# A decoder layer on one core: the recurrence's small products in three groups a chunk in place of six, nine early products, and halved first splits

## Chip, cores, metric

One core of a Trainium2 chip runs the whole program. The metric is device time in microseconds (us) of one execution; the time before is the median of three runs. TensorE is called PE in the profile, VectorE DVE, ScalarE ACT, GpSimd POOL, and SyncE, whose queue issues most transfers, SP.

## The reference

One layer over 1024 tokens of width 1024, in float32. A projection `p = x @ W_in` of 4864 columns is cut into nine parts: q, f, i, g of a gated recurrence (4 heads of 128), q, k, v of a sliding-window attention, and two branch gates of 1024 columns each. Then

```
logf = log(lb + (1 - lb) * sigmoid(f));  k = 1 - exp(logf)
per chunk:  b = cumsum(logf)
  scores[t,s] = sum_k q[t,k] * exp(b[t,k] - b[s,k]) * k[s,k]      (s <= t)
  o = (q * exp(b)) @ state + scores @ v
  state = exp(b_last) * state + (k * exp(b_last - b)).T @ v
o = rms_norm(o) * norm_w * silu(g)
merged = sigmoid(ga) * (o @ W_a) + sigmoid(gb) * (attention @ W_b)
x = layer_norm(alpha * x + merged @ W_out)
x = layer_norm(alpha * x + mixture of 32 experts, two per token, of width 512)
```

## The kernel before

**Numbers.** A float32 operand is split into a high half (ScalarE casts it) and a low half (VectorE subtracts the high one): `split`, line 97. A product of two split operands is three matrix instructions into one PSUM bank (`mm3`, lines 101 to 105: high by high, high by low, low by high; the profile calls them L103, L104, L105). They are called big products here: 128x128 weights, 512 columns. Small products of the recurrence are plain fp32; the trace has two records for each of those products, and one for each transpose.

**Stages.** A Tile planner orders the work: in the first two stages TensorE's instructions run in the order of the program, and the planner orders the other engines' queues by program order and its own estimate of when things are ready. Each engine then executes its queue in that order. After these two stages come mixing (branch products, first norm, router) and the experts, where all five engines keep the order of the program.

*Start* (`att_proj`, line 243). SP issues the loads of x (eight of 512 KB), of the first weights and of constants. `first` (line 265) takes four x chunks in turn: split the chunk (`split_x`), at chunks 0 and 2 split also 512 KB of weights (`wsplit_half`), then issue the products of two of eight k slices for two column tiles: 12 big products a chunk, 48 in all. ScalarE copies each finished column tile out of PSUM (`keep`, L259). Then the second half of x is split and multiplied (`query`).

*Stage 1* computes attention, with the projection for the recurrence as filler. *Stage 2* (from about 303 us to 532 us of the span) computes the recurrence, with the projection of the branch gates as filler: eight columns of weights, 768 big products. `weave` (line 231) deals the filler over the entries of a list: before entry i it issues filler until `start + i * (total - start) / len(main)` units are out. A unit is an estimate of time in the program; the three instructions of one k slice count 0.64. In stage 2 `total` is 164 and `start` is 8.

**The recurrence** (`hgrn`, line 520) goes over eight chunks n of 128 tokens. The lower triangle of the scores is made by levels: at level h (1, 2, 4, ..., 64) each block of 2h tokens gives the products of its later half with its earlier half. `prep_level` makes the operands on ScalarE and VectorE (two exponentials; subtract, two multiplies, add: L571 to L579), each level continuing on the running sums `hl` that the level before it left. `level` and `diag` issue small products of 32 or 64 columns, and `keep` (L538) copies them by a mask into the score tile `hst`, four instructions a level on VectorE. `decay` transposes the decayed keys; `output(n)` multiplies scores by values and queries by the state, then squares on ScalarE, sums on VectorE, takes a power on GpSimd (L701) and scales on VectorE into `ho` (L668); `state(n)` makes the next state; `out(n)` transposes `ho` (L414) and stores it.

These calls stand in a list of groups, sorted by a place: for a chunk n, in this order, levels 1, 2 with the diagonal; output and state of chunk n-1; levels 4, 8; out of chunk n-1; levels 16, 32; level 64 and decay. That is 48 groups. The preparation of a group is issued two groups ahead of it. `load(n + 1)`, five loads of 256 KB, is issued with the preparation of levels 16, 32 of chunk n. Three entries of `mixing_start` (loads and splits for the next stage) are inserted 8, 6 and 4 places from the end, so the list has 51 entries.

**Buffers.** The tiles of the recurrence share one ring of 24 (`s2`); operands of the levels, weights and x share 36 of 4 KB a partition (`q4`); five PSUM banks (`pb`) serve the groups, three (`mm`) the big products.

Of the kernel before, what the change touches and what calls it, by code (L numbers as in the profile page):

```python
# [5 lines left out]
F32 = mybir.dt.float32  # L6
# [55 lines left out]
class Builder:  # L62
# [34 lines left out]
    def split(self, hi, lo, src, eng=None):  # L97
        self.nc.scalar.copy(hi, src)  # L98
        (eng or self.nc.vector).tensor_sub(lo, src, hi.bitcast(F32))  # L99

    def mm3(self, out, lh, ll, rh, rl, start, stop):
        mm = self.nc.tensor.matmul
        mm(out, lh, rh, start=start, stop=False)  # L103
        mm(out, lh, rl, start=False, stop=False)  # L104
        mm(out, ll, rh, start=False, stop=stop)  # L105
# [61 lines left out]
    def split_x(self, half, raws):  # L167

        self.xh.append([])
        self.xl.append([])  # L170
        for raw in raws:
            h, l = self.q4([128, 2, 512], F32R, "xh"), self.q4([128, 2, 512], F32R, "xl")
            self.split(h, l, raw)
            self.xh[half].append(h)
            self.xl[half].append(l)
            yield
# [13 lines left out]
    def wsplit(self, raws):  # L190
        return [self.wsplit_half(raw) for raw in raws]

    def wsplit_half(self, raw):
        h = self.q4([128, 4, 256], F32R, "wh")
        l = self.q4([128, 4, 256], F32R, "wl")
        self.split(h, l, raw)
        return h, l

    def proj_T(self, w, ct, half):
# [43 lines left out]
    def att_proj(self):  # L243
        nc = self.nc
        self.xh, self.xl = [], []
        x0 = [self.load_x(0, 0)]
        raw = [self.wload_half(2048, 0)]
        x0.append(self.load_x(0, 1))
        raw.append(self.wload_half(2048, 1))
        x0 += [self.load_x(0, j) for j in (2, 3)]  # L250
        x1 = [self.load_x(1, j) for j in range(4)]
        raw2 = self.wload(2304)
        self.setup_more()
        raw3 = self.wload(2560)
        self.aq = [self.q4([128, 4, 256], name=f"aq{i}") for i in range(4)]

        def keep(ps, ch, ct, half):
            for b in range(2):
                nc.scalar.activation(self.aq[2 * half + b][:, 2 * ch + ct], ps[:, 256 * b:256 * b + 256], AF.Copy, scale=0.125)  # L259

        def query(w, ch, half):
            for ct in range(2):
                keep(self.run(self.proj_T(w, ct, half)), ch, ct, half)

        def first():

            w, xs = [], self.split_x(0, x0)
            gens = [self.proj_T(w, ct, 0) for ct in range(2)]
            for j in range(4):
                next(xs)  # L270
                if j % 2 == 0:
                    w.append(self.wsplit_half(raw[j // 2]))
                for _ in range(2):
                    for gen in gens:
                        next(gen)
            for ct, gen in enumerate(gens):
                keep(self.run(gen), 0, ct, 0)
            return w

        w = first()  # L280
        for _ in self.split_x(1, x1):
            pass
        query(w, 0, 1)
        w = self.wsplit(raw2)
        for half in range(2):
            query(w, 1, half)
        w = self.wsplit(raw3)
        self.ak = self.q4([128, T], name="ak")
        self.av = self.tile([128, 8, 2, 2, 64], F32R, "av", 1)
        self.ksh = self.tile([128, 2, 2, 128], F32R, "ksh", 1)  # L290
        self.ksl = self.tile([128, 2, 2, 128], F32R, "ksl", 1)
        vts = []
        for half in range(2):
            s = slice(half * 512, half * 512 + 512)
            ps = self.run(self.proj_T(w, 0, half))
            nc.scalar.copy(self.ak[:, s], ps)
            ps = self.run(self.proj_T(w, 1, half))
            vt = self.st2()
            nc.scalar.copy(vt, ps)
            vts.append(vt)  # L300
        for half, vt in enumerate(vts):
            tp = self.bank("pa", (128, 4, 128))
            for i in range(4):
                nc.tensor.transpose(tp[:, i], vt[:, i * 128:i * 128 + 128], self.c("ident"))
            av = self.av[:, 4 * half:4 * half + 4]
            self.split(av[:, :, :, 0], av[:, :, :, 1], tp.rearrange("p i (g d) -> p i g d", g=2))
# [213 lines left out]
    def hgrn(self):  # L520
# [3 lines left out]
        nc = self.nc  # L524
# [15 lines left out]
        def load(n):  # L540
            t0 = slice(n * 128, n * 128 + 128)
            for nm, src in (("hl", self.hl[:, :, t0]), ("hk", self.hk[:, :, t0]), ("hq", self.hq[:, :, t0]),
                            ("hv", self.hv[t0].rearrange("p (h k) -> p h k", h=4)),
                            ("hg", self.hg[t0].rearrange("p (h k) -> p h k", h=4))):
                V[nm, n] = self.tile([128, 4, 128], F32, nm, 2)
                nc.sync.dma_start(V[nm, n], src)
# [6 lines left out]
        def prep_diag(n):  # L553
            V["st", n] = self.tile([128, 4, 128], F32, "hst", 2)
            nc.gpsimd.memset(V["st", n], 0.0)
# [48 lines left out]
        def prep_levels(n, hs):  # L604
            t = self.q4([128, 2, 512], F32, "hE")
            es = [t[:, j].rearrange("p (h x) -> p h x", h=4) for j in range(2)]
            for h, e in zip(hs, es):
                prep_level(n, h, e)

        def levels(n, hs):  # L610

            pp = self.bank("pb", (128, 4, 128))
            posts = [diag(n, pp)] if hs[0] == 1 else []
            posts += [level(n, h, pp, j) for j, h in enumerate(hs)]
            for post in posts:
                post()
# [57 lines left out]
        none = lambda: None  # L674
        groups = []
        for n in range(8):
            at = 4 * n
            groups += [(at, lambda n=n: (prep_diag(n), prep_levels(n, (1, 2))), lambda n=n: levels(n, (1, 2))),
                       (at + 1, lambda n=n: prep_levels(n, (4, 8)), lambda n=n: levels(n, (4, 8))),
                       (at + 2, lambda n=n: (n < 7 and load(n + 1), prep_levels(n, (16, 32))), lambda n=n: levels(n, (16, 32))),  # L680
                       (at + 3, lambda n=n: (prep_levels(n, (64,)), prep_decay(n)), lambda n=n: (levels(n, (64,)), decay(n))),
                       (at + 4.5, none, lambda n=n: (output(n), state(n))),
                       (at + 5.5, none, lambda n=n: out(n))]
        groups.sort(key=lambda t: t[0])
        load(0)
        ahead = 2
        for _, pre, _ in groups[:ahead]:
            pre()

        def group(i):  # L690
            if i + ahead < len(groups):
                groups[i + ahead][1]()
            groups[i][2]()

        return [lambda i=i: group(i) for i in range(len(groups))]

# [748 lines left out]
    def build(self):  # L1445
        pool = self.tc.tile_pool
        with pool(name="base", bufs=1) as self.base, pool(name="dr", bufs=1, space=DRAM) as self.dr:
            self.setup()
            self.n2 = 13
            self.banks = {"mm": 3, "sc": 1, "pa": 3}  # L1450
            with pool(name="sb1", bufs=1, reuse_waits="tile") as self.sb, \
                    pool(name="ps1", bufs=1, space=PSUM, reuse_waits="tile") as self.ps, self.pe_order():
                self.att_proj()
                self.hg_consts()
                stream = self.stream()
                self.weave(self.attention(), stream, 164)
            self.n2 = 24
            self.banks = {"mm": 3, "pb": 5}
            with pool(name="sb2", bufs=1, reuse_waits="tile") as self.sb, \
                    pool(name="ps2", bufs=1, space=PSUM, reuse_waits="tile") as self.ps, self.pe_order():  # L1460
                groups = self.hgrn()
                for n, fn in zip((8, 6, 4), self.mixing_start()):
                    groups.insert(len(groups) - n, fn)
                self.weave(groups, stream, 164, 8)
            self.n2 = 4
            with pool(name="sb3", bufs=1, reuse_waits="tile") as self.sb:
                self.banks = {"mm": 4, "pa": 1, "tb": 1, "pb": 2}
                with pool(name="ps3", bufs=1, space=PSUM, reuse_waits="tile") as self.ps:
                    with self.all_order():
                        self.mixing()  # L1470
                        self.slots()
                    self.overflow()
                self.banks = {"mm": 4, "pb": 4}
                with pool(name="ps4", bufs=1, space=PSUM, reuse_waits="tile") as self.ps, self.all_order():
                    self.moe()
# [44 lines left out]
```

## Time and profile before

| | |
|---|---|
| median of three runs | 1399.96 us (1399.85 to 1399.97) |
| profiled execution | 1399.95 us |
| its span (first to last instruction) | 1398.2 us |
| mean granted TensorE clock | 0.984 |
| PE busy, share of the span | 1335.6 us, 96% |
| weight loads (PEld) | 1100.5 us, 79% |
| VectorE | 1080.5 us, 77% |
| ScalarE | 789.4 us, 56% |
| GpSimd | 241.8 us, 17% |
| transferred | 327.84 MB, mean 234 GB/s |

Times count from the first instruction. Busy times of an engine are the union of its instructions; matrix instructions are pipelined, so their durations overlap: what a stretch of products costs is read from the starts. The page cuts the span into 40 slices of 35 us. Its busy line for TensorE shows 7 tenths in the first slice, 9 or more from there on, and 8, 4, 4 in the last three; VectorE's shows 8 and 9 in slices 4 to 6 (stage 1) and 10 to 14 (most of stage 2), mostly 5 and 6 from there to the experts, and 9 through the experts.

### The profile page before, as it was taken

What the parts mean: (1) busy time and instruction counts of PE and PEld (TensorE: products, weight loads), DVE (VectorE), ACT (ScalarE), POOL (GpSimd) and SP (SyncE); (2) the same over time, 40 slices, a digit from 0 to 9 for tenths busy, and PEclk for the clock granted to TensorE, in tenths of its full rate; (3) what the DMA queues carried; (4) which work ended last, traced back from release to release, by engine and by line L of the source; (5) the groups of instructions that cost most, each with busy time, mean ns of one, the idle gap of its engine ahead of it and who ended that gap; (6) DMA issues with size and microseconds to landing.
All of it is one profiled execution on the core that took longest, in us unless ns stands there. A gap on an engine that the chain in (4) does not pass through costs nothing. (4 is left out here: it accounts for less than half of the span.)

```text
span 1398.2 us, 22818 instructions
## 1 busy us (share of the span) xinstructions
PE 1335.6 (96%) x8314; PEld 1100.5 (79%) x8314; DVE 1080.5 (77%) x1798; ACT 789.4 (56%) x1282; POOL 241.8 (17%) x160
## 2 busy tenths in 40 slices
PE   7999999999999999999998999999999999999844
PEld 5888899987788887788787888888888888888621
DVE  4268985779989956668656989999999999999645
ACT  4367644335545532312112888888888888888542
POOL 0001312120000002300001122222222222222123
PEclk9999999999999999999999999999999999999967
DMA  6124232153444436763557999999999999999962
GB/s 246 56 89 145 100 112 76 39 169 114 137 128 146 148 103 194 254 211 121 196 195 287 356 368 369 366 356 354 353 357 358 352 358 357 367 360 365 369 251 97
DMA packets 142564, 327.84 MB, mean 234 GB/s; under 512 B 18614, under 2 KB 59702, under 8 KB 142448
## 3 DMA queue, kind: packets, MB, share of 16 engines
q1 hardware_dynamic: 132800, 308.78, 60.9%
q0 software_dynamic: 9648, 17.57, 4.9%
q8 instruction: 66, 1.08, 0.3%
q14 instruction: 50, 0.41, 0.1%
HBM read 291.43 MB, written 52.43 MB: 246 GB/s over the span
## 5 line engine op out<-in xcount | busy, mean ns | idle before, releaser
L99 DVE TENSOR_TENSOR el<-er,eh 128x1024 fp32r<-128x1024 f32 x368 | 436.8, 1223 | 53.4 <-ACT eh L98 37.8
L98 ACT CAST eh<-er 128x1024 fp32r<-128x1024 f32 x368 | 369.7, 1054 | 99.5 <-PE mm L104 82.7
L103 PE MATMUL mm<-xh,wh 128*128 128x512 f32 x480 | 194.9, 406 | 7.8 <-ACT wh L98 6.8
L103 PE MATMUL mm<-eh,xh 128*128 128x512 f32 x496 | 196.4, 396 | 0.0
L104 PE MATMUL mm<-el,xh 128*128 128x512 f32 x496 | 196.2, 395 | 0.0
L105 PE MATMUL mm<-eh,xl 128*128 128x512 f32 x496 | 196.1, 395 | 0.0
L104 PE MATMUL mm<-xl,wh 128*128 128x512 f32 x480 | 189.0, 394 | 0.8 <-DVE xl L99 0.8
L105 PE MATMUL mm<-xh,wl 128*128 128x512 f32 x480 | 189.1, 394 | 0.0
L103 PEld LDWEIGHTS mm<-xh,wh 128*128 128x128 f32 x480 | 91.4, 190 | 25.7 <-ACT wh L98 6.8
L105 PEld LDWEIGHTS mm<-eh,xl 128*128 128x128 f32 x496 | 93.2, 188 | 22.5
L104 PEld LDWEIGHTS mm<-el,xh 128*128 128x128 f32 x496 | 93.2, 188 | 22.3
L103 PEld LDWEIGHTS mm<-eh,xh 128*128 128x128 f32 x496 | 93.2, 188 | 22.3
L105 PEld LDWEIGHTS mm<-xh,wl 128*128 128x128 f32 x480 | 91.2, 190 | 20.6 <-DVE wl L99 0.8
L1086 POOL DMA_INDIRECT xg<-x1d,gi x32 | 58.1, 1816 | 279.3 <-PE pb L1149 255.4
L104 PEld LDWEIGHTS mm<-xl,wh 128*128 128x128 f32 x480 | 91.4, 190 | 17.7 <-DVE xl L99 1.1
L103 PE MATMUL mm<-eh,hth 128*128 128x512 f32 x240 | 100.2, 418 | 0.0
L1090 POOL DMA_INDIRECT zd<-y,gi x29 | 69.8, 2407 | 156.5 <-ACT y L1240 156.5
L105 PE MATMUL mm<-eh,htl 128*128 128x512 f32 x240 | 94.8, 395 | 0.0
L104 PE MATMUL mm<-el,hth 128*128 128x512 f32 x240 | 94.8, 395 | 0.0
L103 PE MATMUL mm<-wh,xh 128*128 128x256 f32 x256 | 73.1, 286 | 0.0
L105 PE MATMUL mm<-wh,xl 128*128 128x256 f32 x256 | 72.4, 283 | 0.0
L104 PE MATMUL mm<-wl,xh 128*128 128x256 f32 x256 | 72.4, 283 | 0.0
(257 smaller groups left out, 2522.7 us busy)
## 6 DMA issues: line engine op xcount, KB each, us to landing
er<-w_g SPq DMA_DIRECT2D x128, 512.0 KB
er<-w_u SPq DMA_DIRECT2D x128, 512.0 KB
er<-w_d SPq DMA_DIRECT2D x128, 512.0 KB
wr<-w_in SPq DMA_DIRECT2D x38, 512.0 KB
gated<-st SPq DMA_DIRECT2D x32, 256.0 KB
st<-gated SPq DMA_DIRECT2D x32, 256.0 KB
xr<-xt SPq DMA_DIRECT2D x8, 512.0 KB
wab<-w_a SPq DMA_DIRECT2D x16, 256.0 KB
```

What stands on the lines that cost most here:

```text
L98: self.nc.scalar.copy(hi, src)
L99: (eng or self.nc.vector).tensor_sub(lo, src, hi.bitcast(F32))
L103: mm(out, lh, rh, start=start, stop=False)
L104: mm(out, lh, rl, start=False, stop=False)
L105: mm(out, ll, rh, start=False, stop=stop)
L1086: self.nc.gpsimd.indirect_dma_start(to, None, rows, bass.IndirectOffsetOnAxis(ap=self.column(self.gi, e), axis=0), bounds_check=T - 1, oob ...
L1090: self.nc.gpsimd.indirect_dma_start(self.zd, bass.IndirectOffsetOnAxis(ap=idx, axis=0), y, None, bounds_check=T - 1, oob_is_err=False, com ...
```

## The change

The edit has three parts. A new `early` fills a 128x128 tile with ones and issues nine fp32 products of it with itself into a bank that nobody reads, ahead of `first`. A new `split_parts` splits a tile in two halves along its second dimension, each with its own cast and subtraction; it is used for the first x chunk and the first weight half. The groups of the recurrence are put together in threes a chunk: levels 1, 2 with output and state of chunk n-1; levels 4, 8 with out of chunk n-1; levels 16, 32, 64 with decay. Two more groups end the list, so it has 26, and with the three inserted entries (5, 4 and 2 places from the end) 29. Preparation is still issued two groups ahead; `load(n + 1)` now goes with the preparation of the third group.

```diff
--- before.py
+++ after.py
@@ -98,6 +98,12 @@
         self.nc.scalar.copy(hi, src)
         (eng or self.nc.vector).tensor_sub(lo, src, hi.bitcast(F32))
 
+    def split_parts(self, hi, lo, src):
+
+        n = src.shape[1] // 2
+        for s in (slice(0, n), slice(n, 2 * n)):
+            self.split(hi[:, s], lo[:, s], src[:, s])
+
     def mm3(self, out, lh, ll, rh, rl, start, stop):
         mm = self.nc.tensor.matmul
         mm(out, lh, rh, start=start, stop=False)
@@ -170,7 +176,7 @@
         self.xl.append([])
         for raw in raws:
             h, l = self.q4([128, 2, 512], F32R, "xh"), self.q4([128, 2, 512], F32R, "xl")
-            self.split(h, l, raw)
+            (self.split if half or self.xh[0] else self.split_parts)(h, l, raw)
             self.xh[half].append(h)
             self.xl[half].append(l)
             yield
@@ -190,10 +196,10 @@
     def wsplit(self, raws):
         return [self.wsplit_half(raw) for raw in raws]
 
-    def wsplit_half(self, raw):
+    def wsplit_half(self, raw, first=False):
         h = self.q4([128, 4, 256], F32R, "wh")
         l = self.q4([128, 4, 256], F32R, "wl")
-        self.split(h, l, raw)
+        (self.split_parts if first else self.split)(h, l, raw)
         return h, l
 
     def proj_T(self, w, ct, half):
@@ -262,6 +268,14 @@
             for ct in range(2):
                 keep(self.run(self.proj_T(w, ct, half)), ch, ct, half)
 
+        def early():
+
+            t = self.tile([128, 128], F32, "early", 1)
+            nc.vector.memset(t, 1.0)
+            ps = self.bank("mm")
+            for _ in range(9):
+                nc.tensor.matmul(ps[:, 0:128], t, t, start=True, stop=True)
+
         def first():
 
             w, xs = [], self.split_x(0, x0)
@@ -269,7 +283,7 @@
             for j in range(4):
                 next(xs)
                 if j % 2 == 0:
-                    w.append(self.wsplit_half(raw[j // 2]))
+                    w.append(self.wsplit_half(raw[j // 2], j == 0))
                 for _ in range(2):
                     for gen in gens:
                         next(gen)
@@ -277,6 +291,7 @@
                 keep(self.run(gen), 0, ct, 0)
             return w
 
+        early()
         w = first()
         for _ in self.split_x(1, x1):
             pass
@@ -674,23 +689,21 @@
         none = lambda: None
         groups = []
         for n in range(8):
-            at = 4 * n
-            groups += [(at, lambda n=n: (prep_diag(n), prep_levels(n, (1, 2))), lambda n=n: levels(n, (1, 2))),
-                       (at + 1, lambda n=n: prep_levels(n, (4, 8)), lambda n=n: levels(n, (4, 8))),
-                       (at + 2, lambda n=n: (n < 7 and load(n + 1), prep_levels(n, (16, 32))), lambda n=n: levels(n, (16, 32))),
-                       (at + 3, lambda n=n: (prep_levels(n, (64,)), prep_decay(n)), lambda n=n: (levels(n, (64,)), decay(n))),
-                       (at + 4.5, none, lambda n=n: (output(n), state(n))),
-                       (at + 5.5, none, lambda n=n: out(n))]
-        groups.sort(key=lambda t: t[0])
+            groups += [(lambda n=n: (prep_diag(n), prep_levels(n, (1, 2))),
+                        lambda n=n: (levels(n, (1, 2)), n and (output(n - 1), state(n - 1)))),
+                       (lambda n=n: prep_levels(n, (4, 8)), lambda n=n: (levels(n, (4, 8)), n and out(n - 1))),
+                       (lambda n=n: (n < 7 and load(n + 1), prep_levels(n, (16, 32)), prep_levels(n, (64,)), prep_decay(n)),
+                        lambda n=n: (levels(n, (16, 32)), levels(n, (64,)), decay(n)))]
+        groups += [(none, lambda: (output(7), state(7))), (none, lambda: out(7))]
         load(0)
         ahead = 2
-        for _, pre, _ in groups[:ahead]:
+        for pre, _ in groups[:ahead]:
             pre()
 
         def group(i):
             if i + ahead < len(groups):
-                groups[i + ahead][1]()
-            groups[i][2]()
+                groups[i + ahead][0]()
+            groups[i][1]()
 
         return [lambda i=i: group(i) for i in range(len(groups))]
 
@@ -1459,7 +1472,7 @@
             with pool(name="sb2", bufs=1, reuse_waits="tile") as self.sb, \
                     pool(name="ps2", bufs=1, space=PSUM, reuse_waits="tile") as self.ps, self.pe_order():
                 groups = self.hgrn()
-                for n, fn in zip((8, 6, 4), self.mixing_start()):
+                for n, fn in zip((5, 4, 2), self.mixing_start()):
                     groups.insert(len(groups) - n, fn)
                 self.weave(groups, stream, 164, 8)
             self.n2 = 4
```

## Rows read from the trace of the kernel before

**Rows 1.** Busy us by stretch (instructions): PE, PEld, DVE, ACT, POOL; clock, DMA share, GB/s
```profile
23.20:26.40 3.20, 3.01 (x7) 2.46 (x8) 2.93 (x4) 2.26 (x3) 0.00 (x0) 0.53 0.33 88
...
379.68:460.20 80.52, 80.52 (x1010) 66.05 (x1003) 73.87 (x211) 38.71 (x91) 6.06 (x12) 1.00 0.43 137
...
490.00:530.00 40.00, 40.00 (x397) 33.62 (x384) 22.89 (x66) 12.72 (x26) 2.20 (x3) 1.00 0.28 86
800.00:1300.00 500.00, 500.00 (x2322) 407.37 (x2321) 451.06 (x440) 407.84 (x496) 119.36 (x55) 1.00 0.99 360
```

**Rows 2.** Timeline of the start: start us, duration us, engine, line, operation
```profile
4.43 1.05 ACT L98 CAST xh<-xr 128x1024 fp32r<-128x1024 f32 x1 [2.40 <-DMA xr<-xt]
...
5.67 1.05 ACT L98 CAST wh<-wr 128x1024 fp32r<-128x1024 f32 x1 [0.19 <-DMA wr<-w_in]
...
6.77 0.80 PE L103 MATMUL mm<-xh,wh 128*128 128x512 f32 x1 [6.77 <-ACT wh L98]
...
8.02 0.80 PE L105 MATMUL mm<-xh,wl 128*128 128x512 f32 x1
...
9.05 0.63 PE L104 MATMUL mm<-xl,wh 128*128 128x512 f32 x1
...
9.47 0.63 PE L105 MATMUL mm<-xh,wl 128*128 128x512 f32 x1
...
12.80 1.22 DVE L99 TENSOR_TENSOR wl<-wr,wh 128x1024 fp32r<-128x1024 f32 x1
...
13.23 0.39 PE L105 MATMUL mm<-xh,wl 128*128 128x512 f32 x1
```

**Rows 3.** The same timeline, end of the first block and what follows
```profile
20.74 0.39 PE L105 MATMUL mm<-xh,wl 128*128 128x512 f32 x1
...
22.13 0.50 PE L103 MATMUL mm<-xh,wh 128*128 128x512 f32 x1 [1.00 <-ACT xh L98]
...
23.39 0.80 PE L104 MATMUL mm<-xl,wh 128*128 128x512 f32 x1 [0.76 <-DVE xl L99]
...
26.89 0.39 PE L103 MATMUL mm<-xh,wh 128*128 128x512 f32 x1
```

**Rows 4.** Timeline of PE around three groups: 64 records, 96 records, output with state
```profile
310.04 0.39 PE L105 MATMUL mm<-xh,wl 128*128 128x512 f32 x1
...
311.39 0.39 PE L104 MATMUL mm<-xl,wh 128*128 128x512 f32 x1
...
405.46 0.39 PE L105 MATMUL mm<-xh,wl 128*128 128x512 f32 x1
...
407.08 0.39 PE L104 MATMUL mm<-xl,wh 128*128 128x512 f32 x1
...
410.26 0.39 PE L658 MATMUL pb<-hv,hst 128*128 128x128 f32 x2
...
412.86 0.48 PE L103 MATMUL mm<-xh,wh 128*128 128x512 f32 x1
413.18 0.39 PE L104 MATMUL mm<-xl,wh 128*128 128x512 f32 x1
```

**Rows 5.** VectorE by line, 379.68 to 460.20: busy, mean ns, idle before and releaser
```profile
L99 DVE TENSOR_TENSOR wl<-wr,wh 128x1024 fp32r<-128x1024 f32 x5 | 6.0, 1223 | 0.2 <-ACT wh L98 0.2
L509 DVE TENSOR_SCALAR st<-st 128x512 f32<-128x512 f32 x11 | 4.6, 422 | 0.2 <-ACT st L508 0.2
...
L668 DVE SCALAR_TENSOR_TENSOR ho<-pb,hss,hg 128x128 f32<-128x128 f32 x12 | 3.4, 343 | 3.6 <-POOL hss L701 3.6
```

**Rows 6.** Waits of PE from 303 to 535: total us, times, longest
```profile
PE pb L414 <- DVE ho L668: 1.5, 1, 1.5
...
PE pb L635 <- DVE hkT L623: 0.4, 1, 0.4
```

**Rows 7.** Timeline: last preparation of level 64 of a chunk, and its products
```profile
411.18 0.42 DVE L575 TENSOR_TENSOR hE<-hE,hk 128x256 f32<-128x256 f32 x1
...
428.20 0.68 PE L586 MATMUL pb<-hE 128*64 128x64 f32 x8
```

## The prediction

> **What bounds the kernel now.** I read the table by stretches first, then the timeline of the first 27 us, then the products of single groups in the recurrence stage, then VectorE and the waits there. "Busy" of TensorE hides much: in three whole chunks of the recurrence it is busy 80.52 of 80.52 us, its weight loads 66.05, VectorE 73.87 [rows 1]. So TensorE runs without a gap and VectorE is at 92%: two engines near their limit side by side. From 490 to 530, after the chunks, VectorE is busy only 22.89 of 40 us; in the expert stage TensorE has 500.00 of 500.00 [rows 1]. TensorE's order is fixed, so what it gains or loses early moves all that follows; the transfers of the experts (0.99 of the DMA engines' time) are released by TensorE's progress and move along. I pass shifts to the end one to one.
>
> **The start, now.** The first raw x chunk is cast at 4.43, the first raw weights at 5.67, each for 1.05 us; the first product starts at 6.77, the third at 8.02, when the weights' low half is there [rows 2]. Then products come 0.42 us apart (9.05, 9.47) until about 12.9. The 15th starts at 13.23 and the 48th, the last of this block (two column tiles of 24), at 20.74: 33 steps of 0.228 us [rows 2, 3]. That is the higher of the two clocks, the spacing before it the lower. The block's end releases ScalarE (its copy stands ahead of the next cast), then come a product at 22.13 and, after its low half, one at 23.39; from 23.2 to 26.4 the granted clock is 0.53 [rows 1], and the next eight products take until 26.89 [rows 3].
>
> **Part 1: halved splits and early products.** Halves of the cast: 0.6 us, of the subtraction: 0.7 (estimates, a little over half of 1.05 and 1.22 [rows 2]). The x casts end at 5.65, the first weight half at 6.28, its low half, behind the two of x on VectorE, at 7.1: third product 0.9 us earlier. The nine early products are 18 records of fp32 at full width; such a record takes 2.60/24 = 0.108 us at the higher clock [rows 4], so 0.22 at the lower (estimate: twice), 3.9 us for all; from about 1.1 us, when the tile is filled, to 5.0, in time for 6.28. They add nothing to the path: TensorE idles till 6.77. If they ran half as long again they would end at 6.9 and cost 0.6 of the 0.9.
> Once products come 0.228 apart from about 7.1 to 9.5 on, something else is late: the 27th product needs the low half of the second weights, which VectorE begins at 12.80 and ends at 14.02 [rows 2], behind a transfer and a ScalarE queue that the edit doesn't touch. From there 21 steps of 0.228: the 48th starts at 18.8 in place of 20.74, **1.95 us earlier**, whether the clock rises at 6 or at 10 us. If it doesn't rise before 12.9, the 0.9 us are two products at 0.42, worth 0.5 us later on. The second slow stretch has the same cause as now (two gaps around one product), but with other work before it: from 23.39 to 26.89 stand 8 steps in 3.5 us, which take 1.8 at 0.228, so up to 1.7 us more; VectorE's low halves there, 1.2 us for six products each [rows 2], hold back a little: 1.5. Between 0 and 1.5 I take half. **Start: -2.7 us** (-0.5 to -3.45).
>
> **Part 2: what a group costs TensorE.** No product is added or taken away. Around a 64-record group the last big product starts at 310.04 and the second after it at 311.39; without the group that would be 2 x 0.228 later: 0.90 us extra. A 96-record group (405.46 to 407.08) takes 1.17 extra [rows 4]. So 32 records cost 0.27, and 0.36 us of each small group is start and end, not records. Output and state together are 24 full-width records: 410.26 to 412.86, 2.60 us, and the product after the next comes 0.32 later instead of 0.228: only 0.09 for the switch [rows 4].
> The first merge (levels 1, 2 with output and state) and the second (levels 4, 8 with the transposes of out) save at least 0.09 each and at most 0.36; I take 0.12 and 0.11, nearest to the full-width row. The third joins two small groups, levels 16, 32 and level 64: 0.09 to 0.36, I take 0.30, near the small groups' row. 0.53 us a chunk, eight chunks: **-4.2 us** (-2.2 to -8.6).
>
> **Part 3: pace.** The filler of 164 units is now dealt over 51 places (48 groups, 3 inserts): (164 - 8)/51 = 3.06 units a place; after, over 29: 5.38. A unit is three products in 0.64, 1.067 us. A chunk is six places now, 18.35 units, 19.6 us, and 80.52/3 = 26.84 us in all [rows 1], so groups take 7.26. After: three places, 16.14 units, 17.2 us, plus 6.73: **23.95 us a chunk**. The chunks come closer together and the filler saved is left for the end.
> VectorE needs 73.87/3 = 24.62 us a chunk, of it (6.0 + 4.6)/3 = 3.53 for the filler (low halves, gates), and sits 3.6/3 = 1.2 us behind GpSimd's power before `ho` [rows 1, 5]. At 16.14 units: 21.09 + 3.11 = 24.2 busy, 25.4 with that wait, 26.4 with all 2.2 us of its idle time. So it lacks 0.25 to 2.45 us a chunk, likeliest 1.45; over chunks 1 to 6, 1.5 to 14.7, likeliest 8.7. The place where this lands is `out(n-1)`: its transposes wait for `ho`, which in the order of the program now stands behind all preparations of levels 16 to 64 and decay. Behind them on TensorE queues the filler. It has waited there once already, 1.5 us [rows 6].
> Against it stands a stock: level 64's preparation ends at 411.60 and its product starts at 428.20, 16.6 us later [rows 7]. What VectorE makes that early it can make later without anybody waiting, if `ho` is ordered ahead. Waits: 0 (the stock is used) to 14.7; I take 5, a little over half of the likeliest lack. The waits now, 1.5 and 0.4 before the transposes of `hkT` [rows 6], are part of this and fall away: **+3.1 us**.
> Moved without cost, I say: the five loads of the next chunk, a third of a chunk earlier and before output and state free their buffers (live tiles by my count 22 or 23 of 24); queued behind them on SP are the filler's weights (a column ahead) and gate stores. If they stall, the waits grow toward the upper end above. The inserts (four loads and halvings, then wab and gates) come at 121, 132 and 148 units in place of 130, 140 and 149; VectorE has room there [rows 1], and if not, a halving is 1.2 us [rows 2], 4.9 for four, in chunk 7.
>
> **Sum.** 1399.95 (the profiled execution, span 1398.2 and 1.75 around it; the median is 1399.96) - 2.7 - 4.2 + 3.1 = **1396.1 us**.
>
> **Rivals.**
> *VectorE becomes the bound (slower).* For: 92% now, and a chunk shortened by 11% of its time whose VectorE work shrinks by 2%. The queue runs in order: while `ho` waits 1.2 us, nothing passes it [rows 5]. The Trainium skill ("TensorE: Matmul & The Clock Gate", section "Architectural detail: the array is 16× 32×32, not 1× 128×128") says so too: ScalarE and VectorE are strictly first in, first out; the rows agree. Against: the stock. It decides from the point where the waits exceed 1.9 + 4.2 + 2.7 = 8.8 us; with all 14.7 it gives 1399.95 - 6.9 + 12.8 = 1405.9.
> *Nothing comes of the recurrence.* Waits of 7 to 10 us eat the merges, and the start remains or is half eaten: 1398 to 1401.
> *The stock covers all.* No waits: 1399.95 - 2.7 - 4.2 - 1.9 = 1391.2.
> *The early products don't raise the clock.* Then the start gives 0.5: 1398.4 with the rest as forecast. For: the transition now comes only 6 us after the first product. Against: with halved splits TensorE works without long gaps from 7.1 on.
>
> **Chances.** Forecast (1393.5 to 1398.5) 0.42; VectorE the bound (1401 to 1406) 0.18; nothing (1398 to 1401) 0.20; all covered (1390 to 1393.5) 0.13; clock not raised 0.07. About 0.2%, 2.8 us, is what can be told from no change here, so faster means below 1397.2, slower above 1402.8. Faster: three quarters of the first, all of the fourth, a few hundredths more: 0.49. Slower: nearly all of the second: 0.16. Same: 0.35. Range 1390.5 to 1403.5: it cuts the upper half of the second case and the edge of the fourth, and since cases of both signs count, the forecast's own is 1393.5 to 1398.5.
>
> **What would show it.** Start: the 48th product at 18.8, the third near 7.1, no spacing of 0.42 after 10 us; the stretch after the block with a granted clock of 1.00 or 0.5. Groups: 26 starts in place of 48, chunks 24 us apart where nothing waits, level 64's products directly behind level 32's. Waits: a row "PE pb out <- DVE ho" of 5 us in all; 9 or more and I was wrong in the pace, none and I was wrong in the stock. If the expert stage takes another time than now, the shift didn't pass, and the sum fails for a reason not named here.

## The result, and the profile after

The changed kernel takes **1413.84 us** (median of 4, 1413.06 to 1416.41) against 1399.97 for the kernel before: a ratio of 1.0100, 95% interval 1.0083 to 1.0118. The forecast was 1396.1, with a range that ended at 1403.5. The profiled execution took 1413.26 us, its span is 1411.5.

Where the time went, by the starts of single products in the two profiled executions (us from the span's start):

| | before | after | shift |
|---|---|---|---|
| third product | 8.02 | 7.09 | -0.93 |
| 48th product | 20.74 | 19.03 | -1.71 |
| first product of the recurrence | 305.79 | 303.13 | -2.66 |
| last filler product (end of stage 2) | 531.85 | 544.27 | +12.42 |
| first product of the experts | 767.07 | 780.85 | +13.78 |
| end | 1398.19 | 1411.49 | +13.30 |

So in these two executions the start came out as forecast, and the recurrence stage became 15.08 us longer instead of 1.1 shorter. The experts take the same time in both within 0.5 us, so the shift passed to the end. First the start, in the timeline after (start us, duration us, engine, line, operation; L109 to L111 answer to L103 to L105 of before):

```profile
1.12 3.75 PE L277 MATMUL mm<-early 128*128 128x128 f32 x18 [1.12 <-DVE early L274]
...
4.45 1.14 ACT L98 CAST xh<-xr 128x512 fp32r<-128x512 f32 x2 [2.42 <-DMA xr<-xt]
...
5.69 1.14 ACT L98 CAST wh<-wr 128x512 fp32r<-128x512 f32 x2
...
6.36 0.50 PE L109 MATMUL mm<-xh,wh 128*128 128x512 f32 x1 [1.50 <-ACT wh L98]
...
7.09 0.50 PE L111 MATMUL mm<-xh,wl 128*128 128x512 f32 x1
...
10.48 0.50 PE L110 MATMUL mm<-xl,wh 128*128 128x512 f32 x1 [0.60 <-DVE xl L99]
...
19.03 0.39 PE L111 MATMUL mm<-xh,wl 128*128 128x512 f32 x1
...
21.68 0.50 PE L110 MATMUL mm<-xl,wh 128*128 128x512 f32 x1 [0.77 <-DVE xl L99]
...
23.73 0.40 PE L109 MATMUL mm<-xh,wh 128*128 128x512 f32 x1
```

The eight steps behind the block's end, 23.39 to 26.89 before [rows 3], are 21.68 to 23.73 now: 2.05 us in place of 3.50, at the higher clock. Whether the change did this is taken up below.

Now the recurrence stage. PE's waits from 295 to 560 (total us, times, longest), where before had 1.5 and 0.4 [rows 6]:

```profile
PE pb L429 <- DVE ho L683: 13.1, 5, 5.6
...
PE pb L673 <- ACT hst L613: 0.5, 1, 0.5
```

L429 are the transposes of `out`, and what they wait for is `ho`. The longest of the five waits ends at 340.18. The timeline around it, engine by engine, from the output's products to the transposes, and what the big products do then:

```profile
325.69 1.16 PE L673 MATMUL pb<-hv,hst 128*128 128x128 f32 x8 [0.51 <-ACT hst L613]
...
331.76 1.28 ACT L637 ACTIVATE hkT<-hl 128x128 f32<-128x128 f32 x4 [0.26 <-DVE hl L594]
...
333.59 0.60 ACT L677 ACTIVATE hsq<-pb 128x512 f32<-128x512 f32 x1
...
335.11 2.26 DVE L553 COPY_PREDICATED hst<-lev,pb 32x128 f32<-32x128 int32 x7
337.39 0.69 DVE L679 TENSOR_REDUCE hss<-hsq 128x4 f32<-128x512 f32 x1
...
338.57 1.17 POOL L714 TENSOR_TENSOR hss<-hss,mhalf 128x4 f32<-128x4 f32 x1 [4.22 <-DVE hss L713]
...
339.78 1.13 DVE L683 SCALAR_TENSOR_TENSOR ho<-pb,hss,hg 128x128 f32<-128x128 f32 x4 [0.95 <-POOL hss L714]
...
340.18 1.25 PE L429 MATMUL pb<-const,ho 128*128 128x128 f32 x4 [5.59 <-DVE ho L683]
341.09 0.78 PE L109 MATMUL mm<-xh,wh 128*128 128x512 f32 x1
...
345.50 0.43 PE L110 MATMUL mm<-xl,wh 128*128 128x512 f32 x1
...
395.04 1.25 PE L429 MATMUL pb<-const,ho 128*128 128x128 f32 x4 [4.04 <-DVE ho L683]
```

The output's products are done before 327. Their square is ScalarE's work, and it comes at 333.59, behind the exponentials of levels 16 to 64 and of the decay (331.76 is the last but one). The reduction of the square is VectorE's and comes at 337.39, behind seven masked copies of levels 1 and 2, which follow a queue of preparations. Only then come the power and `ho`. From the start of those products to `ho` it is 14.1 us; TensorE has work for some 9 of them and stands for 5.59.

After it something happens that the prediction does not have at all. From 341.09 to 345.50 ten steps take 4.41 us, 0.44 each, where 0.2275 is the pace of the stage. The table by stretches (us; PE, PEld, DVE, ACT, POOL busy; granted clock; DMA share; GB/s) shows why, and that VectorE was busy for 4.38 of the 5.58 us in which PE stood:

```profile
325.00:341.00 16.00, 9.90 (x133) 8.09 (x120) 14.46 (x39) 7.58 (x18) 3.02 (x4) 0.93 0.47 155
334.60:340.18 5.58, 0.00 (x0) 0.00 (x0) 4.38 (x14) 0.55 (x2) 1.61 (x2) 0.87 0.13 48
338.70:345.60 6.90, 5.42 (x15) 4.22 (x16) 5.62 (x19) 2.24 (x5) 1.52 (x2) 0.51 0.24 76
...
379.68:460.20 80.52, 74.70 (x966) 61.14 (x965) 71.14 (x200) 37.14 (x85) 8.89 (x12) 0.96 0.39 124
```

The granted clock is 0.51 from 338.7 to 345.6: it fell while TensorE stood. A second stretch like it begins at 393.4, within the wait of 4.04 us. Each costs about 2.1 us (4.41 less ten steps of 0.2275). In the window of [rows 1], 379.68 to 460.20, TensorE is busy 74.70 of 80.52 us, where it was busy all the time, and VectorE 71.14 in place of 73.87: it is not more work of VectorE that makes the waits.

### The profile page after: what moved, and what is told of

Its sections match the earlier page's. It is cut to its first block, busy times and chain, and to the rows that moved or that the text cites. A ratio compares the mean times of both kernels' runs of the same rounds, so it can differ in the third digit from the quotient of the medians.

```text
span 1411.5 us, 22864 instructions
## 1 busy us (share of the span) xinstructions
PE 1339.6 (95%) x8332; PEld 1105.5 (78%) x8332; DVE 1084.1 (77%) x1801; ACT 787.0 (56%) x1284; POOL 245.6 (17%) x160
## 5 line engine op out<-in xcount | busy, mean ns | idle before, releaser
L109 PE MATMUL mm<-eh,xh 128*128 128x512 f32 x496 | 196.5, 396 | 0.0
L111 PE MATMUL mm<-eh,xl 128*128 128x512 f32 x496 | 196.1, 395 | 0.0
L109 PE MATMUL mm<-xh,wh 128*128 128x512 f32 x480 | 192.7, 401 | 2.5 <-ACT wh L98 1.5
L111 PE MATMUL mm<-xh,wl 128*128 128x512 f32 x480 | 189.0, 394 | 0.4 <-DVE wl L99 0.4
L111 PEld LDWEIGHTS mm<-eh,xl 128*128 128x128 f32 x496 | 93.2, 188 | 22.5
L109 PEld LDWEIGHTS mm<-eh,xh 128*128 128x128 f32 x496 | 93.3, 188 | 22.2
L109 PEld LDWEIGHTS mm<-xh,wh 128*128 128x128 f32 x480 | 91.6, 191 | 20.5 <-ACT wh L98 1.7
L111 PEld LDWEIGHTS mm<-xh,wl 128*128 128x128 f32 x480 | 91.0, 190 | 20.9 <-DVE wl L99 1.3
L109 PE MATMUL mm<-eh,hth 128*128 128x512 f32 x240 | 100.2, 418 | 0.0
L111 PE MATMUL mm<-eh,htl 128*128 128x512 f32 x240 | 94.8, 395 | 0.0
L109 PE MATMUL mm<-wh,xh 128*128 128x256 f32 x256 | 73.1, 286 | 0.0
L111 PE MATMUL mm<-wh,xl 128*128 128x256 f32 x256 | 72.4, 283 | 0.0
## 6 DMA issues: line engine op xcount, KB each, us to landing
er<-w_d SPq DMA_DIRECT2D x128, 512.0 KB, 11.7
```

## The experiments

The letters of the theories change from one expectation to the next; in the text the theories are named by what they say. The rivals were: *the time* (VectorE needs more of it in a chunk than three short groups leave) and *the order* (`ho` stands too far back in the queues, however much time there is). The kernel before ran again beside each of the three sets of experiments, with medians of 1400.55, 1400.98 and 1399.80; each ratio is against its own set.

**The start alone.** Before's groups, with the new start.

```diff
-            groups += [(lambda n=n: (prep_diag(n), prep_levels(n, (1, 2))),
-                        lambda n=n: (levels(n, (1, 2)), n and (output(n - 1), state(n - 1)))),
...
+            at = 4 * n
+            groups += [(at, lambda n=n: (prep_diag(n), prep_levels(n, (1, 2))), lambda n=n: levels(n, (1, 2))),
...
-                for n, fn in zip((5, 4, 2), self.mixing_start()):
+                for n, fn in zip((8, 6, 4), self.mixing_start()):
```

> The start of the change (early products, halved first splits) with the six groups of before. All theories put the loss in the recurrence, so the recurrence should run as before (waits of TensorE there about 2 us) and the first recurrence product come about 2.7 us earlier: 1397.0 to 1397.6. If the earlier start shifted something later that costs time, 1399 or more.

1400.45 us, ratio 1.0000 (0.9990 to 1.0009). The 48th product stood at 18.39, the recurrence's first at 302.00; the profiled span ended 1.2 us earlier than that of before. What the start gives early is not to be found in the time. In the trace part of it goes behind the recurrence: the recurrence begins 3.79 us earlier than in before's, the experts 1.84 earlier.

**The groups alone.** Before's start, with the three groups.

```diff
-            groups += [(at, lambda n=n: (prep_diag(n), prep_levels(n, (1, 2))), lambda n=n: levels(n, (1, 2))),
...
+            groups += [(lambda n=n: (prep_diag(n), prep_levels(n, (1, 2))),
+                        lambda n=n: (levels(n, (1, 2)), n and (output(n - 1), state(n - 1)))),
...
-                for n, fn in zip((8, 6, 4), self.mixing_start()):
+                for n, fn in zip((5, 4, 2), self.mixing_start()):
```

> The three groups a chunk without the changed start. If the two parts are independent: the changed kernel's time plus 2.7, about 1416.5, with 12 to 15 us of waits before the transposes of out. If the loss came only from both together, it stays near 1400.

1414.16 us, ratio 1.0094 (1.0071 to 1.0116), and the same wait to the tenth: 13.1 us in five, longest 5.6, with low clock from 338.2 and 392.8, 6.8 us each. The whole loss lies in the groups; and without the new start the time is that of the changed kernel, where 2.7 us more were expected.

**Later transposes.** `out(n-1)` goes from the second group of a chunk to the end of the third.

```diff
-(levels(n, (4, 8)), n and out(n - 1))
+levels(n, (4, 8))
...
-(levels(n, (16, 32)), levels(n, (64,)), decay(n))
+(levels(n, (16, 32)), levels(n, (64,)), decay(n), n and out(n - 1))
```

> The changed kernel with out(n-1) moved from the second group of a chunk to the third: its transposes come some 7 us later than in the changed kernel. If the loss is only that the scaling into ho stands too late for a group this near (order), the waits of TensorE fall under 2 us, the low clock in the recurrence goes, and the time is 1396 to 1400. If VectorE can't do a chunk's work in the changed kernel's chunk time (throughput), waits of 6 us or more turn up again, before out or before other products, and it stays at 1404 or more.

1410.78 us, ratio 1.0064 (1.0046 to 1.0082). PE's waits in stage 2 are now:

```profile
PE pb L673 <- ACT hst L613: 8.2, 6, 3.6
PE pb L650 <- DVE ho L683: 2.2, 1, 2.2
```

The waits for `ho` at the transposes are gone, and 8.2 us have come up in their place, at the products of the output, which need the copied scores. That takes away the place of the wait and not its cause: the queues of ScalarE and VectorE are behind, and whichever product comes first to need them waits.

**Output first.** The output and state of the chunk before are issued ahead of levels 1 and 2, and a group's own work ahead of the preparation for the group two places on. The pace stays at 16.14 units a chunk, and VectorE's work is the same.

```diff
-lambda n=n: (levels(n, (1, 2)), n and (output(n - 1), state(n - 1)))
+lambda n=n: (n and (output(n - 1), state(n - 1)), levels(n, (1, 2)))
...
-            if i + ahead < len(groups):
-                groups[i + ahead][0]()
-            groups[i][1]()
+            groups[i][1]()
+            if i + ahead < len(groups):
+                groups[i + ahead][0]()
```

> The changed kernel with output and state ahead of levels 1 and 2 in their group, and each group's products issued before the preparation of the group two ahead, so that the scaling into ho stands ahead of about 9 us of preparations and mask copies in program order. Order theory: waits under 3 us, 1396 to 1400. Throughput theory: the waits move to other products, 6 us or more in all, 1404 or more.

1401.78 us, ratio 1.0013 (0.9998 to 1.0027). Stage 2, from the recurrence's first product to the last filler product, takes 228.4 us instead of 241.1. No wait for `ho` is left; these are:

```profile
PE pb L673 <- ACT hst L613: 3.2, 2, 1.7
PE pb L673 <- DMA gated<-st: 2.3, 1, 2.3
```

and VectorE's work in the stage, up to the first product behind it, is nearly what it was. The first row is the changed kernel's, the second this run's:

```profile
303.13:545.34 242.21, 227.96 (x2706) 187.47 (x2705) 193.91 (x531) 105.63 (x236) 22.45 (x30) 0.97 0.38 124
304.15:533.65 229.50, 223.34 (x2706) 186.22 (x2705) 191.88 (x531) 105.52 (x236) 18.30 (x30) 0.99 0.41 131
```

The same 531 instructions of VectorE, 191.88 us against 193.91, and 12.7 us of stage 2 back. This shows the order to be the larger part. Two edits of the order are in this run together; which of them counts more is not separated.

**The old pace.** The changed kernel with 18.35 filler units a chunk, as before, by a larger total given to the planner (185.4 for 164).

```diff
-                self.weave(groups, stream, 164, 8)
+                self.weave(groups, stream, 185.4, 8)
```

> The changed kernel, but its groups dealt so that a chunk has 18.35 units of filler again, as before (26.6 us a chunk); the last groups get no filler. Theory A (pace: a chunk is shorter than VectorE's work for it): waits before out fall under 3 us, stage 2 takes 225 to 230 us, the time is 1396 to 1401. Theory B (order: the merged groups put the preparations and the mask copies ahead of the scaling in VectorE's queue, whatever the pace): the waits stay at 8 us or more, the time 1408 or more.

1416.31 us, ratio 1.0110 (1.0093 to 1.0127). PE's wait, and one of VectorE's from 295 to 540:

```profile
PE pb L429 <- DVE ho L683: 12.9, 5, 3.4
```

```profile
DVE hl L594 <- ACT hE L586: 13.4, 5, 6.7
```

With 2.2 units, 2.4 us, more for each chunk the waits hardly shrink. This speaks against the time alone, but it does not settle it, since VectorE could not use much of what was added: it stands idle for 13.4 us (3.6 in the changed kernel) because the next chunk's `hl` comes late to ScalarE. One such load leaves SP's queue at 411.75, behind a gated store and two weight loads, and ScalarE waits for it until 416.96. The groups also reach further into the end here, and the last stands behind the last filler product (546.9 against 541.6).

**The quick pace with six groups.** Before with 16.14 units a chunk.

```diff
-                self.weave(groups, stream, 164, 8)
+                self.weave(groups, stream, 145.2, 8)
```

> The kernel before, with its six groups dealt at the changed pace: 16.1 units of filler a chunk. Theory A (pace): waits before out of 6 us or more appear although no group is merged, time 1404 to 1412. Theory B (order by merging): waits stay near 2 us, time within 1 us of 1400.

1408.87 us, ratio 1.0054 (1.0035 to 1.0074). PE's waits in stage 2:

```profile
PE pb L414 <- DVE ho L668: 3.6, 6, 0.8
PE pb L635 <- DVE hkT L623: 1.7, 2, 0.9
PE pb L551 <- DVE hE L575: 0.9, 1, 0.9
```

6.2 us of short waits, none over 0.9, and no low clock in the recurrence. Stage 2 is 7.8 us longer than before. The time around its 48 groups beyond the filler's pace (from the last big product ahead of a group to the second behind it, less two steps of 0.2275) is 67.97 us in place of 60.35, which is nearly all of it. So the time does count: at this pace VectorE is late by a little in most chunks, spread out, with the old order too.

**The multiplication on GpSimd.** One of VectorE's four operations of a preparation moves.

```diff
-            nc.vector.tensor_mul(ev[:, :, 1], ev[:, :, 1], qv[:, :, 1])
+            nc.gpsimd.tensor_mul(ev[:, :, 1], ev[:, :, 1], qv[:, :, 1])
```

> The changed kernel with the query multiply of every level on GpSimd: seven instructions, 2.4 us of VectorE's time a chunk, fewer. Throughput theory: VectorE needs about 23.5 us a chunk against 24, waits fall under 5 us, 1400 to 1405, if GpSimd keeps up (it is 11% busy here; an operation of that size took it 0.41 to 1.8 us). Order theory: waits fall by a fifth at most, 1410 or more.

1424.26 us, ratio 1.0160 (1.0142 to 1.0178): the worst of all. PE's wait (in the profiled execution, at 1429.35 the longest of four), and GpSimd's lines from 300 to 540 (busy, mean ns, idle before):

```profile
PE pb L429 <- DVE ho L683: 16.1, 5, 7.1
```

```profile
L593 POOL TENSOR_TENSOR hE<-hE,hq 128x256 f32<-128x256 f32 x56 | 51.9, 935 | 73.2 <-ACT hE L586 64.6 <-DMA hq<-hqd 6.1 <-ACT hE L589 2.3
L714 POOL TENSOR_TENSOR hss<-hss,mhalf 128x4 f32<-128x4 f32 x7 | 7.6, 1081 | 43.1 <-DVE hss L713 43.1
```

935 ns each, where VectorE takes 420, and `ho`'s own power now stands in one queue with them. The Trainium skill ("Trainium Architecture — The Big Picture", section "The five engines, in one table") puts GpSimd at half of VectorE's speed for streaming elementwise work; 2.2 here agrees. The run does not tell the theories apart.

**Half of the masked copies.** The changed kernel; half of the copies that keep the allowed part of the scores are left out, so that the scores are not the reference's.

```diff
-            for i, b in enumerate(RUNS):
+            for i, b in enumerate(RUNS[:2]):
```

> The changed kernel with half of the masked copies of the scores left out (blocks 2 and 3 of 4): 3.9 us of VectorE's time a chunk fewer, 2 us of it ahead of ho. Throughput theory: no waits left, 1396 to 1399. Order theory: each wait about 2 us shorter, 3 to 6 us left in all.

A single run: 1400.24 us; stage 2 takes 228.4 us, and PE's wait in it is:

```profile
PE pb L429 <- DVE ho L683: 4.2, 3, 3.3
```

VectorE's work in the stage falls from 193.91 to 163.50 us, 3.8 a chunk, and that takes off two thirds of the wait. The copies are also what stands directly ahead of the reduction in the timeline above, so shortening the work shortens the queue; it is no proof for the time against the order.

**Output first, with the inserts folded in.** On top of "output first", the three first parts of the mixing stage go into groups that are there already; the filler is dealt over 26 places, 18 units a chunk.

```diff
-                    groups.insert(len(groups) - n, fn)
+                    k = len(groups) - n
+                    groups[k] = lambda fn=fn, group=groups[k]: (fn(), group())
```

> The changed kernel with two edits: a group's own work is issued ahead of the preparation of the group two places on, with the output and the state of the chunk before ahead of the small levels 1 and 2, so that the copy that makes ho stands early in VectorE's queue; and the three first parts of the mixing stage are folded into groups that are there already, so that the filler is spread over 26 places instead of 29 (18 units a chunk, about the share of the kernel before). Theory A (TensorE waits because ho stands behind preparations in VectorE's in-order queue, and the wait brings the low clock): TensorE's waits for ho in stage 2 fall from 13.1 us to under 2, no stretch of granted clock 0.5 inside the recurrence, and the merges' 2.2 us and the start's 1.6 to 2.7 us are left over: 1395 to 1398 us, ratio 0.997 to 0.999 of the kernel before. Theory B (three groups leave VectorE too little time whatever the order): waits of 4 us and more remain, in other places, 1400 to 1406 us.

**1397.08 us**, ratio 0.9986 (0.9977 to 0.9995): faster than both kernels, by about 2.7 us against before. The chain that took 14.1 us in the changed kernel, in the same chunk:

```profile
325.40 1.06 PE L673 MATMUL pb<-hv,hst 128*128 128x128 f32 x8
...
328.92 0.58 ACT L677 ACTIVATE hsq<-pb 128x512 f32<-128x512 f32 x1
...
329.82 0.68 DVE L679 TENSOR_REDUCE hss<-hsq 128x4 f32<-128x512 f32 x1
...
332.20 1.13 DVE L683 SCALAR_TENSOR_TENSOR ho<-pb,hss,hg 128x128 f32<-128x128 f32 x4 [0.95 <-POOL hss L714]
...
335.25 0.66 PE L429 MATMUL pb<-const,ho 128*128 128x128 f32 x4
```

`ho` comes 6.8 us after the output's products start, and it is there 1.9 us before the transposes come to it. What is left of waits is at the stage's end:

```profile
PE pb L673 <- ACT hst L613: 5.4, 2, 3.8
```

with a granted clock of 0.5 from 511.9 for 6.8 us. The profiled execution took 1401.31 us, the longest of eleven, so how much of this wait the others have is open.

**The same without the new start.**

```diff
-            (self.split if half or self.xh[0] else self.split_parts)(h, l, raw)
+            self.split(h, l, raw)
...
-                    w.append(self.wsplit_half(raw[j // 2], j == 0))
+                    w.append(self.wsplit_half(raw[j // 2]))
...
-        early()
```

> The kernel of the folded groups with output first, but without the nine early products and without the halved splits: the recurrence's part alone, mended. If the start is worth what its own trace shows (the 48th product 1.6 to 2.7 us earlier) this is 1.5 to 2.7 us slower than the same kernel with the start. If the start's gain is lost by the end (the ratio of 1.0000 of the kernel with the start alone says so), the two agree within 1 us. Against the kernel before: the merges' 2.2 us, 1397 to 1399 us.

1397.47 us, ratio 0.9985 (0.9976 to 0.9995). With and without the start the two agree within 0.4 us. PE's waits for the scores at the output's products, 4.1 us in two, are left here too.

**Halved splits alone, and early products alone,** each added to the kernel before.

```diff
-            self.split(h, l, raw)
+            (self.split if half or self.xh[0] else self.split_parts)(h, l, raw)
...
-                    w.append(self.wsplit_half(raw[j // 2]))
+                    w.append(self.wsplit_half(raw[j // 2], j == 0))
```

for the first, and for the second

```diff
+        early()
         w = first()
```

> The kernel before with the halved first splits alone. If the start's gain is from data that come earlier: first product of the projection 0.5 to 1 us earlier, third at about 7.1 us; the 48th at 19.5 to 20 us. If the halves do nothing without the early products, all stays as before: third at 8.0, 48th at 20.6 to 20.8 us (one execution of the kernel before had 19.56).

> The kernel before with the nine early products of a filled tile alone. If the gain of the start is the granted clock: the products from the first one on run at the full clock some us earlier and the 48th product stands at 19 to 19.5 us, with the third still at about 8.0 us. If it is only the earlier data: 48th at 20.6 us as before, and the granted clock of the first 24 us unchanged.

A single run each: 1398.01 and 1401.23 us. With the halves the third product starts at 7.39 and the 48th at 19.24; with the early products at 8.02 and 19.46. Neither decides, because the kernel before varies as much by itself: over the four executions with the old start (before, the groups alone, the quick pace, the folded one without the start) the 48th stands at 20.74, 19.56, 20.60 and 19.64. Over the eight with the whole new start it lies between 18.10 and 19.05, mean 18.74. The means, 20.14 and 18.74, differ by 1.4 us.

## Why the prediction was wrong

**The start held in the trace, step by step, and not in the time.** The early products took 3.75 us (3.9 forecast) and were over at 4.9. The third product came at 7.09 (7.1), the 27th waited for its data till 14.13 (14.02), the 48th came at 19.03 (18.8). The second slow stretch was gone (half of it was forecast). At the recurrence's first product the gain was 2.66 us (2.7). That so much agreed is in part luck, because the execution of before that it is measured against is the latest of the four with the old start. At the 48th product the gain of the means is 1.4 us, and at the recurrence's first product 1.25 (304.35 and 303.10). Nor is the second slow stretch the start's doing: the other three executions with the old start take 2.06 us for its eight steps, while three of the eight with the new one (output first, the old pace, the multiplication on GpSimd) take 2.62 to 3.34. The time shows none of it: 1.0000 with 0.1% either way for the start alone, and 0.4 us between the two folded kernels. A gain of 1.4 us is at the edge of what these intervals exclude; whether it is lost later, as part of it is in the one trace of the start alone, or is only too small to see is not settled.

**"The early products don't raise the clock"** came true in some executions: of nine with early products, six have the big products 0.23 us apart from about 7.4 us on, and three (half of the copies, output first folded, early products alone) only from about 10. It did not matter, as the step said: the 48th stood at 19.03 and 18.88 in the first two, which have the whole start.

**The merges: 4.2 us forecast, about 2.3 measured.** PE around the three merged groups of one chunk after, of which the first and the third are undisturbed:

```profile
436.46 0.39 PE L111 MATMUL mm<-xh,wl 128*128 128x512 f32 x1
436.78 0.46 PE L566 MATMUL pb<-hq,hk 128*32 128x32 f32 x32
...
440.76 0.40 PE L110 MATMUL mm<-xl,wh 128*128 128x512 f32 x1
...
448.04 1.10 PE L429 MATMUL pb<-const,ho 128*128 128x128 f32 x4 [1.17 <-DVE ho L683]
...
454.90 0.39 PE L111 MATMUL mm<-xh,wl 128*128 128x512 f32 x1
...
457.21 0.40 PE L110 MATMUL mm<-xl,wh 128*128 128x512 f32 x1
```

The first takes 4.30 less two steps of 0.23, 3.84 extra. The two groups of before take 1.17 and 2.69, 3.86 together [rows 4]: saved 0.02 (0.12 forecast). The third takes 2.31 less two steps, 1.85; the two of before 0.85 and 1.20 by the same measure: 0.20 (0.30). The second, where nothing waits (365.84), takes 1.28 against 0.90 and 0.45: 0.07 (0.11). That is 0.29 a chunk, 2.3 us in all, at the lower bound of the step (2.2). A join of narrow and wide products saves almost nothing here; that the starting cost moves to where the forms change is my reading and was not tested.

**The waits: +3.1 forecast, +11.7, and +4.2 behind them.** This is the step that failed. 5 us of waits were forecast, 13.6 came in place of 1.9. The rival "VectorE becomes the bound" named the place and the row, and its 14.7 us were nearly right; it had a chance of 0.18. By the prediction's own sign (9 us or more: wrong in the pace) the pace would be to blame; output first, with the same pace, shows that it was mainly the order. Two things in the step were wrong.
First, the stock. I took 16.6 us between a preparation and its product [rows 7] as time that can be lent to `ho`. But a queue that runs in order lends nothing: what is issued ahead of `ho` runs ahead of it, however long its own product can wait. Before, the preparations up to levels 4, 8 of chunk n are issued ahead of output(n-1); after, with two groups ahead being two larger groups, it is all of chunk n, up to decay. "Output first" shows it: the same work of VectorE, at the same pace, another order, and the waits for `ho` are gone. And it is two queues, not one: at 340 ScalarE holds the square for 6.7 us before VectorE holds the reduction for 3.2. The Trainium skill ("TensorE: Matmul & The Clock Gate", section "Architectural detail: the array is 16× 32×32, not 1× 128×128") names both engines as strictly first in, first out; these rows agree, and I had used it for VectorE alone.
Second, the clock. Waits of several us at one place are followed by products at 1.2 GHz: twice 2.1 us after the waits of the changed kernel, none where the same kind of wait comes in pieces under 0.9 us (the quick pace with six groups). So it counted how the waits are dealt out, and their sum was not the whole price.

**Sum by its terms:** start -2.66; stage 2: waits +11.7, low clock +4.2, merges -2.3, and 1.5 that I could put to no row, together +15.08; behind it +0.9. That is +13.3, the difference of the spans. The 1.5 may stand beside the waits: the group whose transposes wait 1.17 us at 448.04 takes 2.97 us beyond the filler's pace, 1.80 without the wait, where an undisturbed one takes 1.28. Some 0.5 us at each of five waits, in place of one, would be 2 us (an estimate).

**The time a chunk** (24.2 to 26.4 us of VectorE in 23.95) was not refuted as a second cause. Six groups at this pace lose 7.8 us of stage 2, and with output first 5.5 us of waits at other products are left. In the folded kernel pace and order are both mended, so its gain can't be dealt out between them. Its 2.7 us are near the merges' 2.3, which is what should be left, but no row shows that they are the merges': in the profiled executions of the two folded kernels, both longer than their medians, stage 2 takes 228.91 and 226.57 us, not less than the 226.06 of before, with 5.4 and 4.1 us of waits in it.

## What to carry to other kernels

Slack between a preparation and its use is worth something only if the work that is late may pass it: in engines that run in order, look for each short chain that crosses engines (here square, reduction, power, scaling), and count what stands ahead of each of its links in each queue. When groups are merged, "two groups ahead" grows with them; set the lead in work, or issue the late chain first. A wait of several us at one spot cost more here than the same in pieces, since TensorE went on at half speed behind it (about 2.1 us more each).

## What I had not expected of the hardware

- Inside a stage where TensorE had run at 1.00 for hundreds of us, waits of 5.6 us at one place were followed by 6.8 us with a granted clock of 0.51; waits of at most 0.9 us were not.
- The same start of the same kernel varies by over 1 us: the 48th product of the old start at 19.56 to 20.74, with products 0.43 us apart until about 10.7 in one and 13.2 in another.
- Joining a group of 32-column products with full-width ones saved 0.02 us of 3.86, joining two groups of narrow ones (32 and 64 columns) 0.20 of 2.05.
- GpSimd's multiplication of 128x256 in fp32: 935 ns against VectorE's 420.
